# Operands of the first gate-building round read from PSUM, and one unit of first products per 16 tokens

## The chip, the cores and the metric

The kernel runs on one core of a Trainium2 chip. The metric is the device time of one execution in microseconds (us). TensorE is called PE, VectorE DVE, ScalarE ACT, GpSimd POOL and SyncE SP, as in the profile.

## The reference

Two small transformers run one after the other on 256 tokens of width 1024. The change lies in the second one's expert layers (two of them, `peer_ffn`). For each token and each of 8 heads, a query is scored against two lists of 128 keys; the 16 best of each list are combined, and the 16 best of the 256 sums give 16 experts per head, out of 128 x 128 = 16384. Each chosen expert adds its row of `v_tab`, weighted with gate x gelu(its row of `u_tab` times the token):

```python
s = jnp.einsum('thpd,hpnd->thpn', q, subkeys).astype(jnp.float32)
s_top, i_top = lax.top_k(s, K)
cand = (s_top[:, :, 0, :, None] + s_top[:, :, 1, None, :]).reshape(PEER_TOK_BLOCK, Hp, K * K)
score, flat = lax.top_k(cand, K)
i1 = jnp.take_along_axis(i_top[:, :, 0], flat // K, axis=-1)
i2 = jnp.take_along_axis(i_top[:, :, 1], flat % K, axis=-1)
expert = i1 * PEER_NKEYS + i2
gate = jax.nn.softmax(score, axis=-1)
h = jnp.einsum('thkd,td->thk', u_tab[expert], zb).astype(jnp.float32)
act = (gate * jax.nn.gelu(h, approximate=False)).astype(zb.dtype)
return jnp.einsum('thk,thkd->td', act, v_tab[expert])
```

## The kernel before

The kernel gathers nothing. It computes gelu(U x) for all 16384 experts, multiplies it by a dense table of gates G (zero where an expert was not chosen) and multiplies the result by V. Experts are taken in 64 chunks `c2` of two units of 128. All large products run as three products of split operands (`mm3`, L338 to L342: high x high, high x low, low x high). A weight unit of 128 x 1024 is loaded by SP (`raw`, four buffers), copied by ACT into its high part `wh` (L335) and subtracted into its low part `wl` (L336) by DVE or, where `eng=GP`, by POOL; `wh` and `wl` have three buffers each.

`u_phase(c2)` (L2124) does the **first products** of one chunk: two units, 2 x 8 x 3 = 48 products into a PSUM bank `mm`, then ACT's gelu into `st`; 40 chunks (`EARLY`, NST = 40) go out to DRAM (`far`) and are fetched again later, the others (`LATE`, the odd ones up to 47) are done shortly before they are needed. `v_phase(c2)` (L2277) does the **second products**: DVE multiplies `st` by G (`sm`), splits the result, and PE adds the products into four PSUM banks, two of the tag `ax`, two of `s`, each tag with two banks.

`peer` (L2104) has these stages for each layer. First the queries and key scores. Then the **routing**, a loop over the two halves `tt` of 128 tokens: DVE's top-16 searches, with a `u_phase` after every second one (24 of the 40 in all, `wl` on POOL); at its end three PE transposes bring first keys, second keys and gates into one `ax` bank `p`, tokens along the columns (L2220). DVE copies them out to SBUF: `i1T` and `i2T` (bf16), and the gates, scaled by 2^14, as a sum of two fp16 numbers in `gp` (L2225 to L2227).

Then **gate building** in four rounds q of 32 first keys each. A round has 16 steps `tg` of 16 tokens (`build_g`, L2234), each in three parts. Part one, on DVE: in round 0 only, `oA` (L2238), the one-hot of the second key, 16 x 128 columns, kept in SBUF for all rounds; `eq` (L2241), the one-hot of the first key within this round's 32; `oB` (L2244), `eq` times the two halves of the gate. Part two: 16 small products on PE into two `tp` banks (L2251), and ACT copies the low half out (`gt`, L2255). Part three, on DVE: the sum of both halves into G (L2260). `eq` and `oB` have two buffers. `advance` moves every step that is under way on by one part and begins a new one. Round 0 runs in the loop at L2306 with a `u_phase` after every odd step, and the units that remain follow it; rounds 1 to 3 run inside the loop over `v_phase`, each one round ahead of its use.

The order on each engine isn't written out: a planner simulates the program with its own costs when the kernel is built, and at each moment gives an engine the earliest instruction in program order that is ready. Each engine then runs its list in that fixed order, with waits. A PSUM bank or SBUF buffer goes to its next owner once its last reader is done.

Of the kernel before, what the change touches and what calls it, by code (L numbers as in the profile page):

```python
# [12 lines left out]
BF16 = mybir.dt.bfloat16  # L13
# [6 lines left out]
OP = mybir.AluOpType  # L20
# [1447 lines left out]
NST = 40  # L1468

LATE = list(range(1, 48, 2))  # L1470
EARLY = [c2 for c2 in range(64) if c2 not in LATE]
# [632 lines left out]
def peer(kk, l, rows, HL, out, dbg):  # L2104
    nc, tc, A = kk.nc, kk.tc, kk.A
    V, SC, PE, GP = nc.vector, nc.scalar, nc.tensor, nc.gpsimd
    ident = kk.ident
    ctx = ExitStack()
    pj = ctx.enter_context(tc.tile_pool(name=f"pp{l}", bufs=1, reuse_waits="tile"))
# [5 lines left out]
    H, L = HL  # L2115

    i1T = pj.tile([128, 256], BF16, name="i1T")
    i2T = pj.tile([128, 256], BF16, name="i2T")
    gp = pj.tile([128, 256, 2], F16, name="gp")
    stp = ctx.enter_context(tc.tile_pool(name=f"ps{l}", bufs=3, reuse_waits="tile"))  # L2120
    stash = {}
# [2 lines left out]
    def u_phase(c2, eng=None):  # L2124
        p = kk.mm()
        for j in range(2):
            h, lo = kk.unit(A["pu"][l, c2 * 2 + j], eng=eng or (GP if j else None))
            for k in range(KD):
                c = slice(k * 128, k * 128 + 128)
                kk.mm3(p[:, j * 256:j * 256 + 256], h[:, c], lo[:, c], H[k], L[k], k == 0, k == KD - 1)  # L2130
        s = stp.tile([128, 512], F32, tag="st", bufs=2, name="st")
        ins = SC.activation(s, p, AF.Gelu).ins
        if c2 == LATE[-1]:
            rows.table(ins)
        if c2 not in LATE:
            far[c2] = kk.dram.tile([128, 512], F32, name=f"far{l}_{c2}")
            SC.dma_start(far[c2], s)
        else:
            stash[c2] = s

    def fetch(c2):
        if c2 in far:
            s = stp.tile([128, 512], F32, tag="sr", bufs=3, name="sr")
            nc.sync.dma_start(s, far[c2])
            stash[c2] = s
# [6 lines left out]
    for q4 in range(4):  # L2152
        ps = [kk.ax(), kk.ax()]
        for j in range(4):
            b = q4 * 4 + j
            p = kk.proj_f(kk.unit(A["wq"][l, b]), H, L, 0, 256)
# [8 lines left out]
    def top16(src, vals, idx):  # L2165
        V.max(vals[:, 0:8], src)
        V.max_index(idx[:, 0:8], vals[:, 0:8], src)
        V.match_replace(src, vals[:, 0:8], src, NEG)
        V.max(vals[:, 8:16], src)
        V.max_index(idx[:, 8:16], vals[:, 8:16], src)  # L2170

    nu = 0
    for tt in range(2):
        vals = rt.tile([128, 16, 16], F32, tag="vals", name="vals")
        idx = rt.tile([128, 16, 16], U32, tag="idx", name="idx")
        for b in range(16):
            top16(sc[tt][:, b, :], vals[:, b, :], idx[:, b, :])
            if b % 2 == 1:
                u_phase(EARLY[nu], GP)
                nu += 1  # L2180
        idf = rt.tile([128, 16, 16], F32, tag="idf", name="idf")
        kk.cv(idf, idx)
        cand = rt.tile([128, 8, 16, 16], F32, tag="cand", name="cand")
        v4 = vals.rearrange("p (h two) k -> p h two k", two=2)
        V.tensor_tensor(cand, v4[:, :, 0, :].unsqueeze(3).to_broadcast([128, 8, 16, 16]),
                        v4[:, :, 1, :].unsqueeze(2).to_broadcast([128, 8, 16, 16]), op=OP.add)
        score = rt.tile([128, 8, 16], F32, tag="score", name="score")
        fl = rt.tile([128, 8, 16], U32, tag="fl", name="fl")
        for h in range(8):
            top16(cand[:, h].rearrange("p a b -> p (a b)"), score[:, h, :], fl[:, h, :])  # L2190
            if h % 2 == 1:
                u_phase(EARLY[nu], GP)
                nu += 1
        i4 = idf.rearrange("p (h two) k -> p h two k", two=2)
        fin = []
        for j in range(2):
            ku = rt.tile([128, 8, 16], U32, tag="ku", name="ku")
            if j == 0:
                V.tensor_scalar(ku, fl, 4, None, op0=OP.logical_shift_right)
            else:  # L2200
                V.tensor_scalar(ku, fl, 15, None, op0=OP.bitwise_and)
            kf = rt.tile([128, 8, 16], F32, tag="kf", name="kf")
            kk.cv(kf, ku)
            V.tensor_tensor(cand, kf[:].unsqueeze(3).to_broadcast([128, 8, 16, 16]),
                            iota[:, 0:16].unsqueeze(1).unsqueeze(1).to_broadcast([128, 8, 16, 16]), op=OP.is_equal)
            V.tensor_tensor(cand, cand, i4[:, :, j, :].unsqueeze(2).to_broadcast([128, 8, 16, 16]), op=OP.mult)
            r = rt.tile([128, 8, 16], F32, tag=f"ie{j}", name="ie")
            V.tensor_reduce(r, cand, axis=AX.X, op=OP.add)
            fin.append(r)
        ge = rt.tile([128, 8, 16], F32, tag="ge", name="ge")  # L2210
        V.tensor_tensor(ge, score, score[:, :, 0:1].to_broadcast([128, 8, 16]), op=OP.subtract)
        SC.activation(ge, ge, AF.Exp)
        gs = rt.tile([128, 8], F32, tag="gsum", name="gsum")
        V.tensor_reduce(gs, ge, axis=AX.X, op=OP.add)
        V.reciprocal(gs, gs)
        V.tensor_tensor(ge, ge, gs[:].unsqueeze(2).to_broadcast([128, 8, 16]), op=OP.mult)
        fin.append(ge)
        p = kk.ax()
        for j, t in enumerate(fin):
            PE.transpose(p[:, j * 128:j * 128 + 128], t.rearrange("p a b -> p (a b)"), ident)  # L2220
        ts = slice(tt * 128, tt * 128 + 128)
        kk.cv(i1T[:, ts], p[:, 0:128])
        kk.cv(i2T[:, ts], p[:, 128:256])
        g = rt.tile([128, 128], F32, tag="gt", name="gt")
        V.tensor_scalar(g, p[:, 256:384], GSC, None, op0=OP.mult)  # L2225
        kk.cv(gp[:, ts, 0], g)
        V.tensor_tensor(gp[:, ts, 1], g, gp[:, ts, 0], op=OP.subtract)  # L2227
    rx.close()


    wk = ctx.enter_context(tc.tile_pool(name=f"pk{l}", bufs=2, reuse_waits="tile"))
    a = wk.tile([128, 256, 128], F8, tag="oA", bufs=1, name="oA")

    def build_g(q, G, tg):  # L2234

        ts = slice(tg * 16, tg * 16 + 16)
        if q == 0:
            V.tensor_tensor(a[:, ts, :], i2T[:, ts].unsqueeze(2).to_broadcast([128, 16, 128]),  # L2238
                            iob[:].unsqueeze(1).to_broadcast([128, 16, 128]), op=OP.is_equal, saturate=False)
        eq = wk.tile([128, 16, 32], BF16, tag="eq", name="eq")  # L2240
        V.tensor_tensor(eq, i1T[:, ts].unsqueeze(2).to_broadcast([128, 16, 32]),  # L2241
                        iob[:, q * 32:q * 32 + 32].unsqueeze(1).to_broadcast([128, 16, 32]), op=OP.is_equal)
        b = wk.tile([128, 16, 2, 32], F16, tag="oB", name="oB")
        V.tensor_tensor(b, eq[:].unsqueeze(2).to_broadcast([128, 16, 2, 32]),  # L2244
                        gp[:, ts, :].unsqueeze(3).to_broadcast([128, 16, 2, 32]), op=OP.mult)
        yield
        parts = []
        for t8 in range(2):
            p = kk.bank("tp")
            for t in range(8):  # L2250
                PE.matmul(p[:, t * 64:t * 64 + 64], a[:, tg * 16 + t8 * 8 + t, :], b[:, t8 * 8 + t].rearrange("p a b -> p (a b)"),  # L2251
                          start=True, stop=True)
            pv = p.rearrange("p (t a j) -> p a j t", t=8, a=2)
            gt = wk.tile([128, 32, 8], F32, tag="gt8", name="gt8")
            SC.activation(gt, pv[:, 1], AF.Copy)  # L2255
            parts.append((pv[:, 0], gt))
        yield
        for t8, (x, gt) in enumerate(parts):
            o = tg * 16 + t8 * 8
            V.tensor_tensor(G[:, :, o:o + 8], x, gt, op=OP.add)  # L2260
# [3 lines left out]
    def advance(new=None):  # L2264

        for x in list(building):
            if next(x, 1):
                building.remove(x)
        if new is not None:
            next(new)  # L2270
            building.append(new)
# [30 lines left out]
    G = wk.tile([128, 32, 256], F32, tag="G", name="G")  # L2302
    for tg in range(18):
        advance(build_g(0, G, tg) if tg < 16 else None)
        if tg % 2 == 1 and nu < NST:
            u_phase(EARLY[nu], GP)  # L2306
            nu += 1
    while nu < NST:
        u_phase(EARLY[nu], GP)
        nu += 1  # L2310
    fetch(0)
    fetch(1)
    for q in range(4):
        Gn = wk.tile([128, 32, 256], F32, tag="G", name="G") if q < 3 else None
        for i in range(16):
            c2 = q * 16 + i
            fetch(c2 + 2)
            if c2 + 1 in LATE:
                u_phase(c2 + 1)
            part = v_phase(c2, G)  # L2320
            if q < 3:
                for tg in BO[i]:
                    advance(build_g(q + 1, Gn, tg) if tg < 16 else None)
        G = Gn
# [46 lines left out]
```

## Time and profile before

| | us |
|---|---|
| median of 3 runs | 3783.75 |
| lowest and highest run | 3782.16, 3784.54 |
| the profiled execution | 3775.62 |
| its span, first to last instruction | 3773.8 |
| PE busy in the span | 3562.2 |
| DVE, ACT, POOL busy in the span | 2777.9, 1753.4, 968.5 |
| mean granted TensorE clock, of full speed | 0.978 |

Times in the rows are us from the span's start, from the one profiled execution. A window gives for each engine its busy time and, in brackets, the number of its instructions. In the order of time, a line is a start, a length, an engine, a line of the kernel, an operation, output <- input, and behind it the idle time before it with what ended it. Matmuls overlap, so the rate of a stretch is read from its count and not from the length of one.

### The profile page before, as it was taken

To read this page: it belongs to the slowest core of one execution; us is meant where nothing else is said; L and a number is where in the kernel's file an instruction comes from. 1 tells how busy PE (TensorE), PEld (TensorE's weight loads), DVE (VectorE), ACT (ScalarE), POOL (GpSimd) and SP (SyncE) were. 2 spreads that over 40 slices of the span, in tenths; PEclk is the share of its full clock that TensorE was granted. 3 is DMA by queue.
4 is the path that set the end of the run, shared out by engine and by line. 5 is a ranking of instruction groups with operands and counts; after the bars stand their busy time and mean duration, and the time that the engine had idled before them with its cause. 6 is when DMAs were issued, how large, how long until landed. Compare 5 with 4: busy or idle time off the path is not lost.

```text
span 3773.8 us, 68763 instructions
## 1 busy us (share of the span) xinstructions
PE 3562.2 (94%) x27715; PEld 3132.6 (83%) x27715; DVE 2777.9 (74%) x4610; ACT 1753.4 (46%) x2844; POOL 968.5 (26%) x487
## 2 busy tenths in 40 slices
PE   8996999999999999998879999999999887999999
PEld 6774878888789888898879888888889887888887
DVE  4674877666878765578897777767557889787776
ACT  4333533256455534544434555553455443455554
POOL 0110425512123110007872111100000687311110
PEclk9998999999999999999989999999999999999999
DMA  6137545543146542355546555664225654656666
GB/s 230 57 104 182 165 132 177 178 136 93 58 151 183 165 149 69 105 182 190 185 157 200 190 192 195 207 213 149 91 90 175 202 174 152 198 187 194 197 195 196
DMA packets 192448, 607.70 MB, mean 161 GB/s; under 512 B 21406, under 2 KB 29312, under 8 KB 191872
## 3 DMA queue, kind: packets, MB, share of 16 engines
q1 hardware_dynamic: 178880, 576.56, 48.6%
q10 hardware_dynamic: 11808, 21.50, 1.5%
q8 instruction: 217, 3.56, 0.4%
q0 software_dynamic: 1440, 5.24, 0.4%
q14 instruction: 103, 0.84, 0.1%
HBM read 575.96 MB, written 27.25 MB: 160 GB/s over the span
## 4 chain that ended last, share of the span: by engine, by line
PE 75%; DVE 18%; DMA 3%; ACT 2%; issue 1%; SPq 0%; POOL 0%; DVEq 0%; ACTq 0%; POOLq 0%
PE mm L340 14%; PE mm L341 13%; PE mm L342 13%; PE ax L340 3%; PE ax L341 3%; PE ax L342 3%; PE s L342 3%; PE s L340 3%; DVE oA L2238 3%; PE s L341 3%; DVE eq L2241 2%; DVE oB L2244 1%; PE tp L2251 1%; DMA raw<-in_w_ada 1%; DVE wl L336 1%
## 5 line engine op out<-in xcount | busy, mean ns | idle before, releaser
L335 ACT ACTIVATE wh<-raw 128x1024 fp32r<-128x1024 f32 (+1 forms) x902 | 947.9, 1053 | 1197.7 <-PE mm L341 686.0
L336 DVE TENSOR_TENSOR wl<-raw,wh 128x1024 fp32r<-128x1024 f32 (+2 forms) x694 | 868.2, 1253 | 460.1 <-ACT wh L335 444.6
L342 PE MATMUL mm<-hl,wl 128*128 128x256 f32 x3120 | 888.8, 285 | 21.5 <-POOL wl L336 21.4
L340 PE MATMUL mm<-hl,wh 128*128 128x256 f32 x3120 | 895.4, 287 | 3.7 <-ACT a L307 2.7
L341 PE MATMUL mm<-hl,wh 128*128 128x256 f32 x3120 | 886.6, 284 | 0.3 <-DVE hl L540 0.3
L336 POOL TENSOR_TENSOR wl<-raw,wh 128x1024 fp32r<-128x1024 f32 x208 | 595.4, 2876 | 934.5 <-ACT wh L335 932.9
L342 PEld LDWEIGHTS mm<-hl,wl 128*128 128x128 f32 x3120 | 594.8, 191 | 30.4 <-POOL wl L336 25.9
L340 PEld LDWEIGHTS mm<-hl,wh 128*128 128x128 f32 x3120 | 594.1, 190 | 21.2 <-issue 10.2
L341 PEld LDWEIGHTS mm<-hl,wh 128*128 128x128 f32 x3120 | 593.7, 190 | 7.1 <-issue 3.5
L340 PE MATMUL mm<-a,wh 128*128 128x256 f32 (+1 forms) x1424 | 471.5, 332 | 15.5 <-ACT wh L335 5.4
L342 PE MATMUL mm<-a,wl 128*128 128x256 f32 (+1 forms) x1424 | 470.6, 331 | 7.6 <-DVE wl L336 7.5
L341 PE MATMUL mm<-a,wh 128*128 128x256 f32 (+1 forms) x1424 | 469.8, 330 | 2.3 <-DVE a L439 2.3
L340 PEld LDWEIGHTS mm<-a,wh 128*128 128x128 f32 x1424 | 271.0, 191 | 47.5 <-ACT wh L335 8.0
L342 PEld LDWEIGHTS mm<-a,wl 128*128 128x128 f32 x1424 | 271.5, 191 | 36.4 <-DVE wl L336 10.5
L341 PEld LDWEIGHTS mm<-a,wh 128*128 128x128 f32 x1424 | 271.7, 191 | 29.2 <-DVE a L439 2.5
L341 PE MATMUL ax<-wl,ah 128*128 128x512 f32 x512 | 201.4, 394 | 0.0
L341 PE MATMUL s<-wl,ah 128*128 128x512 f32 x512 | 199.0, 389 | 0.0
L342 PE MATMUL ax<-wh,al 128*128 128x512 f32 x512 | 191.8, 390 | 0.0
L2244 DVE TENSOR_TENSOR oB<-eq,gp 128x1024 f16<-128x1024 bf16 x128 | 181.5, 1418 | 13.8 <-PE tp L2251 13.8
L342 PE MATMUL s<-wh,al 128*128 128x512 f32 x512 | 191.1, 389 | 0.0
L340 PE MATMUL ax<-wh,ah 128*128 128x512 f32 x512 | 189.9, 401 | 0.0
L340 PE MATMUL s<-wh,ah 128*128 128x512 f32 x512 | 185.2, 390 | 0.0
(577 smaller groups left out, 6162.5 us busy)
## 6 DMA issues: line engine op xcount, KB each, us to landing
raw<-in_pu SPq DMA_DIRECT2D x256, 512.0 KB, 3.7
raw<-in_pv SPq DMA_DIRECT2D x256, 512.0 KB, 3.4
raw<-in_w_in SPq DMA_DIRECT2D x126, 512.0 KB, 3.7
raw<-in_w_up SPq DMA_DIRECT2D x88, 512.0 KB, 4.1
raw<-in_w_ada SPq DMA_DIRECT2D x48, 512.0 KB, 4.7
e<-in_w_ada SPq DMA_DIRECT2D x96, 256.0 KB, 3.1
raw<-in_w_out SPq DMA_DIRECT2D x40, 512.0 KB, 3.6
far<-st ACTq DMA_DIRECT2D x80, 256.0 KB, 3.3
```

What stands on the lines that cost most here:

```text
L335: return (self.nc.scalar.activation(h, x, AF.Copy).ins, (eng or self.nc.vector).tensor_tensor(l, x, h.bitcast(F32), op=OP.subtract).ins)
L336: (eng or self.nc.vector).tensor_tensor(l, x, h.bitcast(F32), op=OP.subtract).ins)
L340: t.matmul(ps, lh, rh, start=first, stop=False)
L341: t.matmul(ps, lh, rl, start=False, stop=False)
L342: return t.matmul(ps, ll, rh, start=False, stop=last).ins
L2238: V.tensor_tensor(a[:, ts, :], i2T[:, ts].unsqueeze(2).to_broadcast([128, 16, 128]), iob[:].unsqueeze(1).to_broadcast([128, 16, 128]), op= ...
L2241: V.tensor_tensor(eq, i1T[:, ts].unsqueeze(2).to_broadcast([128, 16, 32]), iob[:, q * 32:q * 32 + 32].unsqueeze(1).to_broadcast([128, 16, ...
L2244: V.tensor_tensor(b, eq[:].unsqueeze(2).to_broadcast([128, 16, 2, 32]), gp[:, ts, :].unsqueeze(3).to_broadcast([128, 16, 2, 32]), op=OP.mult)
L2251: PE.matmul(p[:, t * 64:t * 64 + 64], a[:, tg * 16 + t8 * 8 + t, :], b[:, t8 * 8 + t].rearrange("p a b -> p (a b)"), start=True, stop=True)
```

## The change

In round 0 of gate building, the three DVE instructions of a step read keys and gates from the transposes' PSUM banks: `banks` keeps both halves' banks `p`. `i2T`, which only round 0 used, is gone. The bank's gate columns are overwritten with the two fp16 halves: after DVE has written them to `gp`, ACT copies each back into the bank (`cs`, 128 columns, into columns 256 to 511), so that `oB` can read both from there. Later rounds read `i1T` and `gp` in SBUF as before. In the loop of round 0 every step is followed by a `u_phase`, until the 40 are done; the loop for the remaining units goes, since sixteen steps take all sixteen.

```diff
     i1T = pj.tile([128, 256], BF16, name="i1T")
-    i2T = pj.tile([128, 256], BF16, name="i2T")
     gp = pj.tile([128, 256, 2], F16, name="gp")
...
     nu = 0
+    banks = []
     for tt in range(2):
...
         kk.cv(i1T[:, ts], p[:, 0:128])
-        kk.cv(i2T[:, ts], p[:, 128:256])
         g = rt.tile([128, 128], F32, tag="gt", name="gt")
         V.tensor_scalar(g, p[:, 256:384], GSC, None, op0=OP.mult)
         kk.cv(gp[:, ts, 0], g)
         V.tensor_tensor(gp[:, ts, 1], g, gp[:, ts, 0], op=OP.subtract)
+        for j in range(2):
+            kk.cs(p[:, 256 + j * 128:384 + j * 128], gp[:, ts, j])
+        banks.append(p)
     rx.close()
...
         ts = slice(tg * 16, tg * 16 + 16)
+        i1, g2 = i1T[:, ts], gp[:, ts, :]
         if q == 0:
-            V.tensor_tensor(a[:, ts, :], i2T[:, ts].unsqueeze(2).to_broadcast([128, 16, 128]),
+
+            o = tg % 8 * 16
+            i1, i2 = (banks[tg // 8][:, j * 128 + o:j * 128 + o + 16] for j in range(2))
+            g2 = banks[tg // 8][:, 256:512].rearrange("p (two t) -> p t two", two=2)[:, o:o + 16, :]
+            V.tensor_tensor(a[:, ts, :], i2.unsqueeze(2).to_broadcast([128, 16, 128]),
                             iob[:].unsqueeze(1).to_broadcast([128, 16, 128]), op=OP.is_equal, saturate=False)
         eq = wk.tile([128, 16, 32], BF16, tag="eq", name="eq")
-        V.tensor_tensor(eq, i1T[:, ts].unsqueeze(2).to_broadcast([128, 16, 32]),
+        V.tensor_tensor(eq, i1.unsqueeze(2).to_broadcast([128, 16, 32]),
                         iob[:, q * 32:q * 32 + 32].unsqueeze(1).to_broadcast([128, 16, 32]), op=OP.is_equal)
         b = wk.tile([128, 16, 2, 32], F16, tag="oB", name="oB")
         V.tensor_tensor(b, eq[:].unsqueeze(2).to_broadcast([128, 16, 2, 32]),
-                        gp[:, ts, :].unsqueeze(3).to_broadcast([128, 16, 2, 32]), op=OP.mult)
+                        g2.unsqueeze(3).to_broadcast([128, 16, 2, 32]), op=OP.mult)
...
     for tg in range(18):
         advance(build_g(0, G, tg) if tg < 16 else None)
-        if tg % 2 == 1 and nu < NST:
+        if nu < NST:
             u_phase(EARLY[nu], GP)
             nu += 1
-    while nu < NST:
-        u_phase(EARLY[nu], GP)
-        nu += 1
     fetch(0)
     fetch(1)
```

## Rows read from the trace of the kernel before

**Rows 1.** The order of time on PE: the first of the second products.

```profile
2011.64 0.40 PE L340 MATMUL ax<-wh,ah 128*128 128x512 f32 x1
```

**Rows 2.** Windows: length, busy PE, PEld, DVE, ACT, POOL (counts); clock, DMA share, GB/s.

```profile
1838.60:2011.60 173.00, 142.84 (x1313) 139.49 (x1312) 157.41 (x96) 67.99 (x99) 131.77 (x42) 0.93 0.52 169
1890.00:1901.50 11.50, 0.02 (x1) 0.02 (x1) 11.50 (x5) 0.00 (x0) 5.94 (x2) 0.55 0.28 91
1901.50:1974.40 72.90, 68.54 (x691) 67.40 (x691) 72.86 (x56) 34.65 (x56) 55.88 (x20) 0.95 0.52 166
2011.60:2500.00 488.40, 488.40 (x3319) 421.62 (x3318) 379.89 (x452) 251.14 (x350) 60.23 (x23) 1.00 0.62 200
3084.30:3257.40 173.10, 142.84 (x1314) 139.50 (x1313) 157.39 (x96) 68.03 (x99) 132.06 (x42) 0.93 0.51 168
```

**Rows 3.** Windows, PE's products into `mm` alone: length, busy (count), clock, DMA, GB/s.

```profile
1838.60:1901.40 62.80, 39.70 (x319) 0.92 0.48 158
1901.50:1974.40 72.90, 62.59 (x483) 0.95 0.52 166
1838.60:2011.60 173.00, 135.61 (x1054) 0.93 0.52 169
1827.80:1850.70 22.90, 22.90 (x195) 1.00 0.65 211
```

**Rows 4.** The chain that ended last, 1975 to 1990: start, us, what.

```profile
1984.61 0.48 PE tp L2251 x16
1985.09 0.20 PE mm L342
```

**Rows 5.** PE's waits from 1838.6 to 2011.6: us in total, times, longest.

```profile
PE tp L2251 <- DVE oB L2244: 13.1, 1, 13.1
PE mm L342 <- POOL wl L336: 10.1, 8, 1.4
PE tp L2251 <- DVE G L2260: 7.0, 7, 2.2
```

**Rows 6.** DVE's instructions by line, whole run: shortest/median/longest in ns, first and last start.

```profile
L2238 DVE TENSOR_TENSOR oA<-i2T,iob x32: 2276/4455/4499, 1842.0 to 3152.6; 128x2048 fp8e4<-128x2048 bf16 x32
L2241 DVE TENSOR_TENSOR eq<-i1T,iob x128: 674/680/2902, 1844.2 to 3647.1; 128x512 bf16<-128x512 bf16 x128
L2244 DVE TENSOR_TENSOR oB<-eq,gp x128: 1209/1218/3429, 1900.2 to 3663.1; 128x1024 f16<-128x1024 bf16 x128
L2260 DVE TENSOR_TENSOR G<-tp,gt x256: 406/414/425, 1914.1 to 3675.7; 128x256 f32<-128x256 f32 x128
L310 DVE COPY a<-mm x39: 411/419/692, 67.0 to 2644.3; 128x256 f32<-128x256 f32 x32, 128x384 f32<-128x384 f32 x4, 128x512 f32<-128x512 f32 x3
```

**Rows 7.** The order of time on DVE around the first gate group.

```profile
1839.71 2.38 DVE L2227 TENSOR_TENSOR gp<-gt,gp 128x128 f16<-128x128 f32 x1
...
1854.23 46.06 DVE L2238 TENSOR_TENSOR oA<-i2T,iob 128x2048 fp8e4<-128x2048 bf16 x11
1900.22 1.21 DVE L2244 TENSOR_TENSOR oB<-eq,gp 128x1024 f16<-128x1024 bf16 x1
```

**Rows 8.** The order of time on POOL, before and beside the run of `oA`.

```profile
1836.61 2.40 POOL L336 TENSOR_TENSOR wl<-raw,wh 128x1024 fp32r<-128x1024 f32 x1 [0.42 <-ACT wh L335]
...
1849.34 46.61 POOL L336 TENSOR_TENSOR wl<-raw,wh 128x1024 fp32r<-128x1024 f32 x11
```

**Rows 9.** ACT's copies by line, whole run: shortest/median/longest in ns.

```profile
L307 ACT ACTIVATE o<-s x24: 258/278/278, 169.2 to 1034.3; 128x128 f32<-128x128 f32 x24
L2255 ACT ACTIVATE gt<-tp x256: 363/378/390, 1902.1 to 3674.4; 128x256 f32<-128x256 f32 x128
```

**Rows 10.** The chain that ended last, 1790 to 1845: the first half's gates.

```profile
1795.03 0.20 DVE gt L2225
...
1803.14 0.22 DVE gp L2227
```

**Rows 11.** The transposes' line: PE idle before them, us and times, until.

```profile
  DVE ie L2208: 65.2, 8
```

## The prediction

> **What bounds the kernel now.** I read the windows by stage first, then PE's waits, then DVE's and POOL's order of time. In each expert layer the sixteen steps of the first round of gate building, with the first products (the `mm` products of `u_phase`) left over from the routing before, fill a stretch of 173.0 us: from the last transpose of the routing at 1838.6 to the first of the second products (`ax`) at 2011.6 [rows 1]; in the second layer it is 173.1 us [rows 2]. After it PE is busy for all of 488.4 us at a granted clock of 1.00 [rows 2]: the work behind the stretch is bound by PE, so what the stretch loses, the run loses.
>
> How much does it lose? A clean stretch at its edge, 1827.80 to 1850.70, most of it before DVE begins on the gates, does 195 first products in 22.90 us: 0.1174 us each [rows 3]. The stretch holds 1054 [rows 3]: 1054 x 0.1174 = 123.8 us. To these come sixteen groups of gate products (`tp`), 0.48 us each, and about 0.08 us more for the product behind a group (0.20 us) [rows 4]: 16 x 0.56 = 9.0 us. PE needs 132.8 us; the other **40.2 us** per layer are lost. PE's waits name 13.1 + 10.1 + 7.0 = 30.2 us of them [rows 5]: once for the first `oB`, eight times for POOL's `wl`, seven times for DVE's `G`. The remaining 10 us go to products at the lower clock level (1.2 in place of 2.4 GHz) behind waits: in 1890.00 to 1901.50, where PE stood still, the granted clock was 0.55 [rows 2].
>
> All three waits have one cause. DVE is busy for 157.4 of the 173.0 us [rows 2], and its instructions come in two lengths: `oA` 2276 ns at least and 4455 in the median, `eq` 674 to 2902, `oB` 1209 to 3429 [rows 6]. POOL's `wl` takes 2.40 us while DVE waits for the transposes, but eleven of them took 46.61 us, 4.24 each [rows 8], beside eleven `oA` in 46.06 us, 4.19 each [rows 7]: the two engines take turns. These three DVE instructions read two SBUF tensors. `G` reads one tensor from PSUM and one from SBUF, and ran 256 times within 406 to 425 ns [rows 6], those of this stretch beside POOL's 131.8 us of work [rows 2]. A PSUM input, then, is what spares an instruction the turn.
>
> The Trainium skill ("SBUF — State Buffer", section "Who interferes with whom") gives the reason: a DVE instruction with two SBUF inputs shares a read port with GpSimd as an exclusive lock, one with at most one SBUF input does not. By that rule the trace agrees: `G` at 425 ns at most, `oA` doubled [rows 6].
>
> **The change, part by part.**
>
> *Operands from PSUM.* In round 0 `oA`, `eq` and `oB` each get one input from the transposes' bank, so each should keep its shortest length: 16 x 2.28 + 16 x 0.68 + 16 x 1.21 + 32 x 0.41 = 79.9 us of DVE work per layer, in place of about 150. That is under PE's 132.8, so DVE leaves the path, and POOL falls back to 2.40 us per `wl` [rows 8] (two per unit: 4.8 us against PE's 48 x 0.1174 = 5.64). The read itself: nothing in the trace does these three from PSUM. A copy from PSUM takes 692 ns for 512 columns at most [rows 6], so `oA` (2048) lies between 2.28 and 4 x 0.69 = 2.77 us; I take 2.28, since `G` from PSUM (406 ns for 256) costs no more per column than `oA` does. At 2.77 DVE's sum is about 91 us, still covered.
>
> The Trainium skill ("VectorE: DVE Perf Modes", section "The perf-mode tier table") speaks against the change: a tensor_tensor on bf16 in SBUF runs at 2x, with any PSUM operand at 1x, 1224 ns against about 2293 for 2048 columns. Here `oA` takes 2276 ns from SBUF, 1x already, so there is no tier to lose; by that rule each `oA` would have lost an estimated 1.07 us.
>
> *The first gate group.* DVE's order has thirteen `oA` and two `eq` before the first `oB` (two of each in turn where the dots stand, then eleven `oA` [rows 7]). From the end of the last `gp` instruction, 1839.71 + 2.38 = 1842.1, this takes 13 x 2.28 + 2 x 0.68 = 31.0, and `oB` 1.2 more: 1874.3, where now it is 1901.4 [rows 7]. PE's order has 319 first products before its first gate product [rows 3], 37.5 us: PE gets there at 1876.1, so the 13.1 us wait goes, with 1.8 us to spare. At 2.77 us per `oA` PE would wait about 5 us. If that order is planned anew, the first `oB` can only move ahead of more `oA`.
>
> *Two copies per half by ACT* (`cs` from `gp` into the bank), eight in all, 0.26 to 0.28 us each by ACT's copy of 128 x 128 out of PSUM, at most 0.39 by `gt`'s 256 columns [rows 9]: 2 to 3 us of ACT in the whole run, which is busy 68 of the 173 us [rows 2]. I cost them at nothing: the cover is PE's three buffers of weights. What they add is a wait: the second copy needs DVE's `gp` instruction, and behind it in ACT's queue stand the `wh` of the next units. In the first half that instruction ends at 1803.4, though `gt` stood ready at 1795.2 [rows 10]: ACT could stand up to 8.1 us; in the second half from 1838.6 to 1842.1, 3.5 us. Together 0 to 11.6 us per layer; I take 0, because the routing has PE stand still for the transposes' inputs anyway (65.2 us in eight waits over both layers [rows 11]), and in the second half two buffers of weights (2 x 24 products, 5.6 us) can lie ready.
>
> *The cast of i2T* goes, four on DVE, each of about the 0.20 us that the next instruction on as many columns takes [rows 10]: worth 0 to 0.8 us; taken as 0. The banks are held until the last `oB` of round 0; who wants them next is the first `ax` product, which needs `G` of all 256 tokens and so comes later anyway.
>
> *One unit per 16 tokens* moves seven units per layer from behind the loop into it; no instruction is added, and on SP and ACT the order of loads and stores stays that of the units. The total for PE is the same. What it takes away is the work behind the loop that covered the last gate group on its way through ACT and DVE into `sm` and `al` (about 4.1 us: `tp` 0.48, two `gt` of 0.38 [rows 9], two `G` of 0.41, and for `sm` and the two halves of its split, 512 columns each, at most 0.69 apiece by the copy of that width [rows 6]). The cover that is left is `u_phase(1)`, issued before `v_phase(0)`: 5.6 us. So nothing is exposed; without it 4 us per layer.
>
> *What is late next.* Round 1's `eq` and `oB` still read SBUF twice, and the first two groups (two `oB` buffers) can be built beside the last units. One clash costs 3.43 - 1.21 = 2.2 us [rows 6]; I take one per layer.
>
> **The sum.** 40.2 - 2.2 = 38.0 us per layer, 76.0 for two. The profiled execution took 3775.6 us (span 3773.8); 3699.6 after. It ran 0.2% under the median of 3783.75; with the same 76.0 us taken off, the median comes to **3708 us**. Without any clash and with all 40.2 us back, 3703; with the copies' and the operand's far ends (23.2 + 9.6) charged in full, 3741.
>
> **The rivals.**
>
> *A: the collision returns.* DVE, done early, runs ahead into round 1, whose instructions read SBUF twice. For: it has about 50 us to spare per layer. Against: round 1's gate products stand behind all units of round 0 in the program, and only two `oB` buffers exist. Price: in 1901.50 to 1974.40 such instructions run beside POOL, and PE does 691 products [rows 2], of them 483 first products [rows 3] and so thirteen gate groups, worth 56.7 + 7.3 = 64.0 us, in 72.9: a rate of 0.88. For half of the 132.8 us that costs 9 us per layer, for all of it 18. Gain 62 down to 44: 3722 to 3740.
>
> *B: it does not do what it says.* The `G` rows are spared for another reason than the PSUM input, and DVE's stretch stays as long. The units are then only reordered: 3784, within 0.2%. Against: 256 rows of `G` without one exception.
>
> *C: slower, by ACT's queue.* Place: the copies into the bank, ahead of `wh`. Price: 11.6 us per layer, 23 in all, if no buffer covers it: 3807 where B holds as well. It decides once less than 11.6 of the 40.2 us come back. Against: PE has up to three buffers of weights ahead, and in the routing it is DVE that ends last.
>
> **How the numbers follow.** Forecast 0.68 (3700 to 3716), A 0.20, B 0.05, C 0.07. The predicted time is the forecast's, 3708. The range 3699 to 3742 holds the forecast and A and leaves B and C out. Differences under 0.2% (7.6 us) cannot be told from none here. Faster 0.88 (forecast and A), same 0.05 (B), slower 0.07 (C).
>
> **What would show it.** Right: every `oA` near 2.28 us, and in round 0 `eq` near 0.68 and `oB` near 1.21; POOL's `wl` at 2.40 between the transposes and the first `ax`; no wait of PE for the first `oB`; that stretch 133 to 138 us in both layers; the PE-bound 488 us behind it unchanged. Wrong: `oA` still at 4.4 (B); `wl` at 2.8 to 3.1 with round 1's `eq` at 2.2 inside the stretch (A); ACT idle before a copy of `gp` with PE waiting for `wh` or `wl` (C); or a wait for `oB` that remains because PE's order brings the first gate product earlier.

## The result, and the profile after the change

The changed kernel takes 3720.64 us (median; 3717.38 to 3727.02) beside 3782.95 us (3781.84 to 3784.54) for the kernel before: a ratio of 0.9837, 95% interval 0.9820 to 0.9854. That is faster by 62.3 us, within the range given (3699 to 3742) and 12.6 us over the time given, 3708. The profiled execution took 3717.38 us, span 3715.6 us; between the two profiled executions the gain is 58.2 us.

The gain lies in the stretch that the prediction named. On PE the last transposes of the routing end at 1838.49 us, within 0.2 us of before, and the first of the second products starts 29 us sooner than in [rows 1]. The first line is from PE's order of time, with the wait ahead of it in brackets; the others are windows (length; busy us and count of PE, PEld, DVE, ACT, POOL; clock, DMA share, GB/s):

```profile
1982.50 0.79 PE L340 MATMUL ax<-wh,ah 128*128 128x512 f32 x1 [1.18 <-ACT ah L335]
```

```profile
1838.49:1982.50 144.01, 138.00 (x1351) 136.71 (x1349) 88.71 (x96) 71.40 (x106) 101.16 (x43) 0.98 0.67 215
1849.50:1960.00 110.50, 110.50 (x1072) 109.80 (x1071) 57.63 (x61) 55.40 (x79) 87.78 (x38) 1.00 0.69 222
1960.00:1982.50 22.50, 16.49 (x188) 15.89 (x186) 20.18 (x28) 10.67 (x19) 4.40 (x2) 0.87 0.56 186
1982.50:2470.00 487.50, 487.50 (x3292) 420.37 (x3293) 377.18 (x450) 247.37 (x344) 61.15 (x23) 1.00 0.62 198
3053.50:3197.55 144.05, 138.04 (x1352) 136.74 (x1350) 88.71 (x96) 71.44 (x106) 101.18 (x43) 0.98 0.67 215
```

Against [rows 2] the stretch fell from 173.0 to 144.0 us, in the second layer from 173.1 to 144.0; DVE's work in it fell from 157.4 to 88.7 us, POOL's from 131.8 to 101.2 for about as many instructions. The stage behind it is bound by PE as before, but it starts at the lower clock. These are PE's first 4 us in it (length; busy, count; clock, DMA share, GB/s), in the kernel before and in the changed one:

```profile
2011.60:2015.60 4.00, 4.00 (x20) 1.00 0.76 227
1982.50:1986.50 4.00, 4.00 (x16) 0.50 0.23 70
```

The last part of the run, from the second layer's first `ax` to the end, where the clock was the same 0.50 at first, takes 518.05 us and took 516.40; the part between the two stretches is 1.7 us shorter. Twice 29 us is then nearly the whole 58.2 us between the profiled executions.

DVE's three instructions in the whole run and POOL's `wl` in the first layer's stretch, by line (shortest/median/longest in ns), for [rows 6] and [rows 8]:

```profile
L2245 DVE TENSOR_TENSOR oA<-ax,iob x32: 2273/2283/2284, 1841.7 to 3180.7; 128x2048 fp8e4<-128x2048 f32 x32
L2248 DVE TENSOR_TENSOR eq<-ax,iob x32: 672/679/682, 1843.9 to 3182.9; 128x512 bf16<-128x512 f32 x32
L2251 DVE TENSOR_TENSOR oB<-eq,ax x32: 1202/1221/1222, 1846.7 to 3187.6; 128x1024 f16<-128x1024 bf16 x32
```

```profile
L336 POOL TENSOR_TENSOR wl<-raw,wh x41: 2388/2402/2427, 1843.3 to 1965.2; 128x1024 fp32r<-128x1024 f32 x41
```

The reader is to see two things: the three instructions keep their shortest length of before, to within 13 ns, in every one of their 32 executions; and POOL's `wl`, 4.24 us each beside `oA` before, takes 2.4 us every time.

But 144.0 us is not the 135.0 that the forecast makes of it (173.0 - 38.0). What PE waits for in the stretch (us in total, times, longest), for [rows 5], and the products into `mm` in the windows' last part:

```profile
PE tp L2258 <- DVE G L2267: 4.8, 3, 2.8
PE ax L340 <- ACT ah L335: 1.2, 1, 1.2
```

```profile
1838.49:1982.50 144.01, 131.04 (x1078) 0.98 0.67 215
1960.00:1982.50 22.50, 13.11 (x108) 0.87 0.56 186
```

The waits for `oB` and `wl` are gone. The stretch now holds 1078 first products and seventeen gate groups (272 gate products by sixteen; the seventeenth is round 1's first): 1078 x 0.1174 + 17 x 0.56 = 136.1 us of work by the prediction's prices, so 7.9 us are lost. Seven of them lie in the last 22.5 us, which hold 108 products and five groups: 108 x 0.1174 + 5 x 0.56 = 15.5 us of work. From 1849.5 to 1960 (880 products and twelve groups, 110.0 us of work in 110.5) next to nothing is lost. The end, in PE's order of time (all but the first products):

```profile
1971.49 0.64 PE L2258 MATMUL tp<-oB,oA 128*128 128x64 f16 x16
1974.11 0.72 PE L2258 MATMUL tp<-oB,oA 128*128 128x64 f16 x16 [0.36 <-DVE G L2267]
1977.64 1.01 PE L2258 MATMUL tp<-oB,oA 128*128 128x64 f16 x16 [2.81 <-DVE G L2267]
1980.31 1.01 PE L2258 MATMUL tp<-oB,oA 128*128 128x64 f16 x16 [1.65 <-DVE G L2267]
```

After 1974 PE has gate groups alone: each waits until DVE's `G` has emptied a bank of the group before, and the first `ax` waits for the last `G` of round 0 on its way through `sm` and `ah`. DVE, idle for much of the stretch, is busy for 20.2 of these 22.5 us: round 1's `eq` and `oB` and the `wl` of the next weights, which DVE makes here, stand between the `G`. The group of 1974.11 was ready for its `G` at 1975.8, when ACT's two `gt` ended, but its `G` stood in DVE's queue until 1977.18:

```profile
1975.15 0.65 ACT L2262 ACTIVATE gt<-tp 128x256 f32<-128x256 f32 x2
```

```profile
1974.31 0.68 DVE L2248 TENSOR_TENSOR eq<-i1T,iob 128x512 bf16<-128x512 bf16 x1
1974.91 1.21 DVE L336 TENSOR_TENSOR wl<-raw,wh 128x1024 fp32r<-128x1024 f32 x1
1976.04 1.21 DVE L2251 TENSOR_TENSOR oB<-eq,gp 128x1024 f16<-128x1024 bf16 x1
1977.18 0.74 DVE L2267 TENSOR_TENSOR G<-tp,gt 128x256 f32<-128x256 f32 x2
```

Why the groups stand so late is to be read in DVE's order of time, once the gates have begun:

```profile
1875.82 1.22 DVE L2251 TENSOR_TENSOR oB<-eq,ax 128x1024 f16<-128x1024 bf16 x1 [21.04 <-PE tp L2258]
1876.96 2.28 DVE L2245 TENSOR_TENSOR oA<-ax,iob 128x2048 fp8e4<-128x2048 f32 x1
1879.16 0.68 DVE L2248 TENSOR_TENSOR eq<-ax,iob 128x512 bf16<-128x512 f32 x1
1879.76 0.74 DVE L2267 TENSOR_TENSOR G<-tp,gt 128x256 f32<-128x256 f32 x2
1883.45 1.22 DVE L2251 TENSOR_TENSOR oB<-eq,ax 128x1024 f16<-128x1024 bf16 x1 [2.95 <-PE tp L2258]
```

DVE no longer does thirteen `oA` ahead of the first `oB`, as in [rows 7]: from the third `oB` on it does one per group, then waits 2.95 us of every 7.63 for PE. PE's list is built with 60 first products (7.0 us) between two groups, so PE and not DVE sets the pace. The planner wrote a new order for the changed kernel. Counted in the programs as built, and found the same in PE's order of time in the traces, the first products that stand ahead of the end of each gate group in PE's list of the first expert layer:

```
before        319 74 35 34 34 34 34 34 34 34 34 34 34 35 34 34 | the rest behind
after         310 60 60 60 60 61 34 60 60 60 60 60 60 60 13  0  0
all oA ahead  373 40 40 40 40 40 34 40 47 48 48 48 48 48 48 48 48
```

At one group per 60 products the products run out two to three groups too early. The last line is that of an experiment below.

### The profile page after: what moved, and what is told of

Its sections match the earlier page's. It is cut to its first block, busy times and chain, and to the rows that moved or that the text cites. A ratio compares the mean times of both kernels' runs of the same rounds, so it can differ in the third digit from the quotient of the medians.

```text
span 3715.6 us, 68805 instructions
## 1 busy us (share of the span) xinstructions
PE 3550.2 (96%) x27715; PEld 3124.4 (84%) x27715; DVE 2639.0 (71%) x4606; ACT 1754.0 (47%) x2852; POOL 904.0 (24%) x487
## 4 chain that ended last, share of the span: by engine, by line
PE 82%; DVE 11%; DMA 3%; ACT 2%; issue 1%; POOL 0%; SPq 0%; DVEq 0%; ACTq 0%; POOLq 0%
PE mm L340 16%; PE mm L342 15%; PE mm L341 15%; PE ax L340 4%; PE ax L341 3%; PE ax L342 3%; PE s L340 3%; PE s L342 3%; PE s L341 3%; PE tp L2258 2%; DMA raw<-in_w_ada 1%; DVE wl L336 1%; PE ax L1094 1%; PE s L1750 1%; PE tp L1773 1%
## 5 line engine op out<-in xcount | busy, mean ns | idle before, releaser
L336 POOL TENSOR_TENSOR wl<-raw,wh 128x1024 fp32r<-128x1024 f32 x208 | 531.0, 2560 | 941.9 <-ACT wh L335 912.4
L336 DVE TENSOR_TENSOR al<-sm,ah 128x512 fp32r<-128x512 f32 x128 | 127.5, 996 | 30.2 <-ACT ah L335 29.5
```

The lines of the kernel that those rows point to most:

```text
L336: (eng or self.nc.vector).tensor_tensor(l, x, h.bitcast(F32), op=OP.subtract).ins)
```

## The experiments

The theory at the start (T): the operands carry the gain; what is missing is lost at the end of the stretch, where the last gate groups have no products beside them. Rivals were that the units' order carries part of it, that ACT's copies cost something, and, for the end, that the chain of the last group alone, the low clock, or a `wl` on DVE is the loss.

**The operands without the moved units.** The changed kernel with the loop of before:

```diff
-        if nu < NST:
+        if tg % 2 == 1 and nu < NST:
             u_phase(EARLY[nu], GP)
             nu += 1
+    while nu < NST:
+        u_phase(EARLY[nu], GP)
+        nu += 1
```

> The changed kernel with the old loop: operands from PSUM, but a unit only after every odd step and the rest behind the loop. Theory T (the 9 us per layer that are missing from the forecast are lost at the end of the stretch, where no first product is left to cover the last gate groups): the seven units behind the loop cover the end, PE does not wait there, the stretch falls to 136 to 138 us and the run to 3703 to 3712. Rival U (one unit per step is what keeps PE and DVE in step; without it DVE runs many oA ahead and PE waits for the first oB and for G): the run comes out above the changed kernel, 3725 to 3745.

Measured: 3712.86 us (3711.95 to 3720.43), ratio 0.9824, interval 0.9806 to 0.9841; the stretch 141.8 us and 141.6 us. The operands alone give all of the gain; moving the units adds none to it. But the theory had expected the seven units behind the loop to cover the end, a stretch of 136 to 138 us and no wait there, and that did not come: the planner spaces the groups by 60 products here too and leaves 34, 27 and 0 ahead of the last three, and PE still waits for `G` there, for 3.3 us. The stretch loses about 5.4 us by the same prices, where the changed kernel (13, 0 and 0) loses 7.9.

**The moved units without the operands.** The kernel before with the changed loop (the reverse of the diff above).

> The kernel before with one unit per step and nothing else: all operands from SBUF. Theory T (the PSUM operands carry the gain, because DVE and POOL no longer take turns): oA, eq and oB keep their long durations (4.4, 2.2 to 2.9, 1.2 to 3.4 us), DVE stays the bound of the stretch, 3770 to 3790. Rival U (the order of the units carries the gain): 3720 to 3745 with the long durations still there.

Measured: 3773.26 us (3767.22 to 3779.03) beside 3779.68, ratio 0.9983, interval 0.9971 to 0.9995, a stretch of 170.4 us, and 171.8 in the second layer. PE's waits for `oB` and `wl` are those of [rows 5]:

```profile
PE tp L2251 <- DVE oB L2244: 13.1, 1, 13.1
PE mm L342 <- POOL wl L336: 10.2, 8, 1.4
PE tp L2251 <- DVE G L2260: 4.5, 3, 2.2
```

So the reordering touches neither the wait for the first `oB` nor those for `wl`; by itself it is worth 0.2% (6 us).

**Is it POOL that doubles `oA`?** The kernel before, all operands in SBUF, with the `wl` of round 0's units given to DVE instead of POOL:

```diff
-            u_phase(EARLY[nu], GP)
+            u_phase(EARLY[nu], V)
...
-        u_phase(EARLY[nu], GP)
+        u_phase(EARLY[nu], V)
```

> The kernel before with the low parts of the units in the loop of round 0 and behind it made by DVE in place of POOL; operands from SBUF as before. If taking turns with POOL is what doubles DVE's instructions, oA, eq and oB are short (2.28, 0.68, 1.21 us) wherever POOL is idle, although both inputs lie in SBUF; DVE then has about 80 + 39 us of work in the stretch, and the run takes 3725 to 3755. If reading SBUF twice is slow by itself, the long durations stay and the run gets slower than before, above 3790.

Measured: 3759.15 us (3756.43 to 3769.09), ratio 0.9944, interval 0.9926 to 0.9961: four microseconds over the range expected. The mechanism is confirmed by the row of `oA`, which reads the same two SBUF tensors as before and falls to its short length in the median. POOL still has the last `wl` of the routing's units when the gates begin; the second and third lines split the first layer's sixteen `oA` at the end of that work, 1876.8 (those before it, those after it):

```profile
L2238 DVE TENSOR_TENSOR oA<-i2T,iob x32: 2277/2279/4496, 1849.1 to 3139.7; 128x2048 fp8e4<-128x2048 bf16 x32
L2238 DVE TENSOR_TENSOR oA<-i2T,iob x6: 2278/4465/4491, 1849.1 to 1874.5; 128x2048 fp8e4<-128x2048 bf16 x6
L2238 DVE TENSOR_TENSOR oA<-i2T,iob x10: 2278/2279/2282, 1878.9 to 1901.0; 128x2048 fp8e4<-128x2048 bf16 x10
```

```profile
1849.50 27.33 POOL L336 TENSOR_TENSOR wl<-raw,wh 128x1024 fp32r<-128x1024 f32 x7 [0.45 <-ACT wh L335]
```

With POOL idle all ten are short; beside POOL's `wl` five of six are long, and the short one had begun before a `wl` did. The size was missed because the work itself went to DVE: PE waits 13.8 us for the first `oB` and 7.9 us for a `wl` that stands in DVE's queue.

**Which operand?** The changed kernel with `oA` alone reading the bank; no copies by ACT:

```diff
-            i1, i2 = (banks[tg // 8][:, j * 128 + o:j * 128 + o + 16] for j in range(2))
-            g2 = banks[tg // 8][:, 256:512].rearrange(...)[:, o:o + 16, :]
+            i2 = banks[tg // 8][:, 128 + o:144 + o]
...
-        for j in range(2):
-            kk.cs(p[:, 256 + j * 128:384 + j * 128], gp[:, ts, j])
```

> The changed kernel with one operand alone taken from the bank: oA reads its indices from PSUM; eq and oB read i1T and gp from SBUF as before the change, and ACT copies nothing into the bank. It says how the gain divides among the three operands. Of the DVE time above the shortest lengths in the stretch of the kernel before, oA has 15 x (4.03 - 2.28) = 26 us, eq 16 x (2.23 - 0.68) = 25 us, oB 15 x (1.95 - 1.21) = 11 us. Theory S (what counts is only whether DVE and POOL each stay under PE's 136 us; with oA short, the collisions that are left fit beside PE): 3710 to 3725 us, a stretch of 139 to 145 us. Theory M (each collision delays a wl, and each delayed wl stops PE, as the eight waits of the kernel before did): eq and oB keep more than half of the loss: 3735 to 3755 us, a stretch of 150 to 160 us, waits of PE for wl.

Measured: 3722.57 us (3719.14 to 3724.36), ratio 0.9845, interval 0.9830 to 0.9860, a stretch of 143.4 us in both layers: the time of the full change. Yet the other two still collide. Groups of DVE and POOL from 1850 to 1975 us (busy us, mean ns; idle before):

```profile
L2245 DVE TENSOR_TENSOR eq<-i1T,iob 128x512 bf16<-128x512 bf16 x18 | 33.7, 1874 | 0.0
L2248 DVE TENSOR_TENSOR oB<-eq,gp 128x1024 f16<-128x1024 bf16 x17 | 31.2, 1834 | 17.6 <-PE tp L2255 17.6
L2242 DVE TENSOR_TENSOR oA<-ax,iob 128x2048 fp8e4<-128x2048 f32 x14 | 31.0, 2278 | 0.0
L336 POOL TENSOR_TENSOR wl<-raw,wh 128x1024 fp32r<-128x1024 f32 x39 | 99.4, 2552 | 27.1 <-ACT wh L335 26.9
```

`eq` and `oB` take 1.87 and 1.83 us in the mean, against 0.68 and 1.22 from the bank, but DVE (121.8 us of 143.4 busy) and POOL (107.0 us) stay under PE, and no wait for `wl` is left. Yet the equal time does not show that these collisions are free. PE's order here is a better one: in the trace its groups stand 48 products apart from the sixth on, and the end loses 1.9 us for `ah` alone. What that order gives is lost again near 1892 and 1912, where DVE, in a row of long `eq` and `oB`, is late with `G`. PE's waits, and DVE's order of time ahead of the first one:

```profile
PE tp L2255 <- DVE G L2264: 4.4, 2, 3.0
PE ax L340 <- ACT ah L335: 1.9, 1, 1.9
```

```profile
1887.89 3.07 DVE L2248 TENSOR_TENSOR oB<-eq,gp 128x1024 f16<-128x1024 bf16 x1
1890.99 0.69 DVE L2245 TENSOR_TENSOR eq<-i1T,iob 128x512 bf16<-128x512 bf16 x1
1891.60 3.38 DVE L2248 TENSOR_TENSOR oB<-eq,gp 128x1024 f16<-128x1024 bf16 x1
1894.91 0.74 DVE L2264 TENSOR_TENSOR G<-tp,gt 128x256 f32<-128x256 f32 x2
```

So an engine that is under the bound for the whole stretch can still be over it for a part. What `eq` and `oB` cost in one and the same order, no run shows.

**Without the gates' copies.** As above, but `oA` and `eq` both read the bank, `oB` reads `gp`.

> The changed kernel without ACT's copies of the gates into the bank: oA and eq read the bank, oB reads eq and gp from SBUF as before the change. It prices the third operand and the copies. Theory T (an instruction with two SBUF inputs takes turns with POOL: oB 1.2 to 3.4 us and each such wl 2.2 longer; POOL then needs 22.5 units x 4.8 + 16 x 2.2 = 143 us of a stretch of 136 to 144): between 0 and 20 us more than the changed kernel, oB's median between 2.2 and 3.5 us. Rival C (the copies hold ACT's queue and cost time): less than the changed kernel, by up to 23 us, and no loss from oB.

Measured: 3719.74 us (3713.87 to 3722.22) beside 3724.81 for the changed kernel on the same chip, a stretch of 140.5 us in both layers. `oB` did grow, to 2227 ns in the mean of the same window, and the time fell: the theory missed the sign. The run does not show that the copies cost anything: the changed kernel has no wait for ACT in its stretch but the last one for `ah`. In the order built here the last groups stand 48 products apart and the end loses less; that the gain is that order's is read from the trace and not tried by itself. Two waits for `G`, 1.2 us in all, are new in mid-stretch, the first behind two `oB` of 3.0 and 2.9 us.

**The end of the stretch: fewer units first.** The changed kernel with no units after the first two steps (`if tg >= 2 and nu < NST`).

> The changed kernel with its sixteen units on steps 2 to 17 in place of 0 to 15, so that two units stand behind the last gate products. Theory T (the end of the stretch is uncovered): PE's waits for G and ah at the end (6 us per layer, and the lower clock behind them) go, 3704 to 3712. Rival (PE waits at the end for another reason, such as DVE's wl of the first late unit): unchanged, 3717 to 3724.

Measured: 3714.69 us (3710.45 to 3718.18), ratio 0.9824, interval 0.9807 to 0.9841; a stretch of 142.2 us, and of 141.6 in the second layer, with waits for `G` of 3.6 us there. A small part of the end came back, less than expected. PE's order in the trace is that of the run of the operands without the moved units, 34, 27 and 0 products ahead of the last groups, so the two runs are one test and not two.

**The end of the stretch: units held back.** The last two units of each layer go into the loop of the second products:

```diff
-        if nu < NST:
+        if nu < NST - 2:
             u_phase(EARLY[nu], GP)
             nu += 1
...
             part = v_phase(c2, G)
+            if nu < NST:
+                u_phase(EARLY[nu], GP)
+                nu += 1
```

> The changed kernel, but the last two units of first products of each layer are issued in the loop of the second products, one behind each of the first two v_phase calls; the work is the same. In the order as built, PE's list now ends the stretch with 16, 29, 22, 2 and 22 products between the last gate groups, where the changed kernel has its last five groups with 60, 60, 13 and then 0 products between them; but the stretch holds the same products. Theory T (the 8 us per layer are lost because the last gate groups stand bunched behind the last products, with nothing for PE to do while DVE and ACT finish them): part of it comes back only if products lie between the last groups or behind them; expected 5 to 12 us less than the changed kernel beside it. Rival U (the loss is the chain of the last group alone, ACT's two gt, two G, sm and its split, about 4 us, whatever stands ahead of it): 0 to 3 us less, since that chain still stands alone at the end. Rival W (the loss is the low clock's and not the bunching's): no difference.

The changed kernel once more, as the measure for this run, the one above without copies and the next:

> The changed kernel once more, as the measure for the three kernels beside it on the same chip. Expected: 3715 to 3723 us (3720.6 before), the stretch from the last routing transpose to the first second product 144 us in both layers, 8 of them lost, 7 of these in its last 22 us.

Measured: 3735.87 us (3733.59 to 3743.84), against 3724.81 (3722.72 to 3726.54) for the changed kernel (2 us over what was expected of it, with the expected stretch of 144.0): 11 us slower, which none of the theories expected. The products into `mm`, whole stretch and its last 22.5 us:

```profile
1840.48:1985.93 145.45, 127.45 (x1030) 0.98 0.63 204
1963.43:1985.93 22.50, 8.22 (x48) 0.84 0.33 113
```

The stretch lost 48 products (5.6 us of work) and got longer, not shorter. The planner put half of the 96 held products behind the second products' start and none behind the last groups; less work was left beside the last groups, and the end grew. That speaks for T in reverse.

**The order that the prediction assumed.** The changed kernel, but all sixteen `oA` are issued ahead of the gate building:

```diff
     G = wk.tile([128, 32, 256], F32, tag="G", name="G")
+    for tg in range(16):
+        o = 128 + tg % 8 * 16
+        V.tensor_tensor(a[:, tg * 16:tg * 16 + 16, :], banks[tg // 8][:, o:o + 16]..., iob[:]..., op=OP.is_equal, ...)
     for tg in range(18):
```

> The changed kernel, but all sixteen oA of a layer are issued in a loop of their own ahead of the gate building; nothing else differs. In the order as built PE's list has its first gate group after 373 products and then one group per 40 to 48 products to the end, with one group behind the last product (the changed kernel: one per 60 products, four to five at the end). This is the order that the prediction assumed DVE would keep. Theory T (bunched groups at the end are the loss): the stretch falls from 144 to 137 to 140 us per layer, 8 to 14 us less than the changed kernel in all. Rival U (the chain of the last group alone is the loss): the same time as the changed kernel within 4 us. Rival V (the first group comes late and PE waits for the first oB, as in the kernel before): a wait of 1 to 6 us for oB in each layer, which eats the gain.

Measured: 3710.65 us (3701.89 to 3711.28), 14.2 us under the changed kernel beside it, ratio to before 0.9796, interval 0.9776 to 0.9816. The stretch is 138.3 us in both layers, at a clock of 1.00; its windows (all engines, then the products into `mm`), the only wait of PE in it, and the end in PE's order of time:

```profile
1841.62:1979.92 138.30, 136.43 (x1351) 135.58 (x1350) 91.00 (x96) 69.96 (x106) 101.11 (x43) 1.00 0.69 220
1957.42:1979.92 22.50, 20.62 (x221) 20.34 (x221) 14.73 (x18) 11.84 (x20) 9.38 (x4) 1.00 0.69 219
```

```profile
1841.62:1979.92 138.30, 130.85 (x1078) 1.00 0.69 220
```

```profile
PE ax L340 <- ACT ah L335: 1.9, 1, 1.9
```

```profile
1964.98 0.64 PE L2256 MATMUL tp<-oB,oA 128*128 128x64 f16 x16
1971.19 0.64 PE L2256 MATMUL tp<-oB,oA 128*128 128x64 f16 x16
1977.40 0.64 PE L2256 MATMUL tp<-oB,oA 128*128 128x64 f16 x16
1979.92 0.50 PE L340 MATMUL ax<-wh,ah 128*128 128x512 f32 x1 [1.88 <-ACT ah L335]
```

The work is the same, 1078 products and seventeen groups; spread one per 48 products, the groups find products beside them to the end, and 2.2 us are lost where it was 7.9. This decides for T: the chain of the last group still stands alone and costs 1.9 us, the wait for `ah`; the other 5.7 us and the low clock go with the bunching. The rival of the `wl` on DVE fails as well: `wl` stand among DVE's last instructions here too, and no group waits. But DVE has only 14.7 us of work in the last 22.5 here, after 20.2, so PE's spacing and DVE's load at the end changed together, and the runs do not part them. The wait for the first `oB` that rival V expected is absent.

It was run again with, beside it, the same order without the gates' copies:

> The kernel with all oA ahead once more, beside the two others on one chip. Expected: 13 to 15 us under what the changed kernel gave against the same kernel before, a ratio of 0.978 to 0.982, a stretch of 138.3 us in both layers.

> All sixteen oA ahead of the gate building, as in oa_ahead, and no copies of the gates into the bank, as in no_copies: oA and eq read the bank, oB reads gp. In the order as built PE's list has its first gate group after 377 products, then one per 34, later per 48 products, one behind the last product. Theory T (the order of the gate groups is what the end costs; with oA out of the way DVE and POOL have slack enough for the collisions of oB): the same time as oa_ahead beside it within 5 us, 3704 to 3714 us, a stretch of 137.5 to 139.5 us. Rival (the collisions of oB with wl stop PE again): waits of PE for wl, a stretch above 142 us, 3715 to 3735 us.

Measured: 3715.09 us (3702.65 to 3717.85), ratio 0.9818 (0.9801 to 0.9836), and 3711.58 us (3705.66 to 3714.55), ratio 0.9816 (0.9803 to 0.9829), with stretches of 138.3 and 138.4 us. The two can't be told apart: where the order leaves slack, the third operand and the copies are worth nothing either way. Both have the shortest stretches here. The second time the gain over the changed kernel was smaller: 13 to 15 us were expected, and the ratios of 0.9818 and 0.9837 are 7 us apart, with intervals that overlap; only the first time did the changed kernel run beside it, and there no run of the one reached the other.

## Why the prediction was right, and where it was 9 us per layer short

**The bound and the cause: right.** The stretch, the three waits and their one cause hold. Every `oA` at 2.28 us, `eq` at 0.68, `oB` at 1.22, `wl` at 2.4 and no wait for `oB` or `wl`: each of the marks set for "right" is there except the stretch's length and the unchanged stage behind it, which the low clock at its start makes 1.6 us longer. The Trainium skill's rule on who interferes with whom ("SBUF — State Buffer", section "Who interferes with whom") agrees on both sides: one operand moved to PSUM frees `oA` (2283 ns, after 4455), and so does the other engine's absence (2279 ns with `wl` on DVE).

**The price of the PSUM operand: right.** It was taken at 2.28 us for `oA` out of 2.28 to 2.77; measured 2.283 at the median. The reason given for that choice does not hold: `G` takes 406 ns for 256 columns, 1.59 ns per column, and `oA` 2276 for 2048, 1.11, so `G` costs more per column and not "no more". The choice within the range was lucky.

**The operands' shares: not asked.** The prediction summed all three. The run with `oA` alone has the same stretch, but by another way: `oA` alone ends the waits for the first `oB` and for `wl`, the collisions that are left come with 4.4 us of waits for `G`, and a better order at the end makes up for them.

**Rivals.** A (the collision returns) is not seen: `wl` at 2.4 us. Nor is the clash of 2.2 us per layer that the sum charged. B is refuted by the rows of `oA`. C (ACT's queue) cost nothing: the last transposes end at 1838.49, where they ended at 1838.6, and taking the copies out of the better order left the stretch at 138.4 us.

**The step that failed: the end of the stretch.** "The cover that is left is `u_phase(1)` ... So nothing is exposed" priced the end at zero, and at 4 us without the cover. It measured 7 of the 7.9 us lost per layer. It goes back to the sentence on the order of the first gate group, "If that order is planned anew, the first `oB` can only move ahead of more `oA`": it did so, and that was not harmless. With `oA` inside each group the planner set one group per 60 products, three groups were left when the products ran out, and each needs its own turn through PE, ACT and DVE, on a DVE that is busy for 20.2 of the last 22.5 us. "DVE leaves the path" holds for the sum of the stretch and not for its end. The prediction counted work per engine for the whole stretch and the chain of one group at its end; it did not ask how far apart the groups would stand.

**The sum, redone.** Forecast 135.0 us per layer, measured 144.0. Of the 9.0 us, 7.9 - 2.2 = 5.7 are loss, nearly all at the end, in place of the clash; 0.6 is the seventeenth group, which only changed sides; 2.8 are 24 first products (half a chunk) that came from the routing ahead of it, from its last transposes' front to behind them. In the first layer the routing ends at the same time without them, so there they are a loss; in the second, PE does 4004 products from one layer's first `ax` to the next layer's last transpose where it did 4029, in 1071.0 us after 1072.7, so part of them may have come back:

```profile
1982.50:3053.50 1071.00, 528.34 (x4004) 0.99 0.53 171
```

Twice 9 us is the 17.8 us by which the gain between the profiled executions fell short (76.0 against 58.2); the medians, with a difference of 62.3, fell short by less, since the profiled execution of before was 0.2% under its median. The far end of the sum is 0.5 us too high by its own numbers (13 x 0.49 - 1.8 = 4.6 us per layer for the operand, 9.1 and not 9.6), which changes nothing. With all `oA` ahead, as the prediction had assumed of thirteen of them, the loss per layer is 2.2 us. That this equals the clash of 2.2 us that the sum charged is chance: no clash stopped PE, and the 2.2 are nearly all the last group's chain. That kernel's medians, 3710.65 and 3715.09, lie 3 and 7 us over the 3708 forecast.

**What stays open.** Why the planner spaces the groups by 60 products in one kernel and by 48 in another was read from its orders, not tried: DVE waits for PE in both, 2.95 us per group in the changed kernel, so DVE's real durations do not ask for it. Why it moves half a unit out of the routing is open as well.

## What to carry to other kernels

Where DVE and POOL double each other's instructions, first take one input of the longest instruction from PSUM and see whether both engines come under the one that bounds the stage. What collisions are left may then be free or not: `oB`'s were, once the order left slack; `eq`'s and `oB`'s together came with 4.4 us of waits in a part of the stretch. When a wait goes that used to hold one engine's work back, look at the order that will be planned anew: count the bounding engine's work between the pieces of the slower chain, down to the last one, because pieces left over when the filler is used up are paid in full, one chain each, together with whatever else stands in the slower engine's queue there. A unit held back to cover an end may be placed behind it, so the order as built is read before such a cover is believed.

## What the runs showed of the hardware

Reading `oA`'s indices as f32 from PSUM cost no more than reading them as bf16 from SBUF: 2283 ns at the median against 2279 with POOL out of the way. With both inputs in SBUF, in the run with `wl` on DVE, the same instruction took 4.45 to 4.50 us wherever a `wl` of POOL was already under way, and 2.28 in all twenty executions with POOL idle. The Trainium skill ("VectorE: DVE Perf Modes", section "The perf-mode tier table") gives a bf16 tensor_tensor in SBUF twice the rate of one with a PSUM operand; no such difference is seen in this instruction, whose SBUF form was at the lower rate already. The granted clock fell to 0.87 in the 22.5 us where PE stood between gate groups, and was still 0.50, the lower of the two levels (1.2 and 2.4 GHz), in the first 4 us of work behind them; it stayed at 1.00 through the whole stretch where the groups were spread.
